# A 128-byte gap in SBUF between the weight ring and the activation pools of a transformer kernel

## The chip, the cores and the metric

The kernel runs on one core of one Trainium2 chip. The metric is device time in microseconds (us), lower is better: the median of three runs of the kernel before is 1367.99 us (1367.96 to 1368.49).

## What is computed

The input is one sequence of 256 tokens with 1024 features, all in fp32. It passes through a first block (a gated feed-forward network of width 2816; a mixer that joins a gated linear recurrence and windowed attention; a second feed-forward network) and then twice through a second kind of layer, with a convolution branch, a latent attention branch, a dilated attention branch and an output projection:

```python
def swiglu(x, w_gu, w_down):
    g, u = jnp.split(x @ w_gu, 2, axis=-1)
    return (jax.nn.silu(g) * u) @ w_down
...
        f = swiglu(rms_norm(h, ffn1_pre_g[l]), ffn1_w_gu[l], ffn1_w_down[l])
        h = h + MACARON_SCALE * rms_norm(f, ffn1_post_g[l])
        m = hybrid_mixer(rms_norm(h, mix_pre_g[l]), cos, sin, w_in[l], ...)
        h = h + rms_norm(m, mix_post_g[l])
...
    merged = g_a * (y_a @ w_out_a) + g_b * (y_b @ w_out_b) + g_c * (y_c @ w_out_c)
    return x + merged @ w_o
```

Nearly all of the arithmetic is in the products of the 256-token activations with weight matrices, 227 MB of weights in all, each used once.

## The kernel before, in words

**Matmuls.** Each fp32 product is done as three fp32r matmuls (`mm3`, L221 to L225): an operand x is split into a rounded high part and a remainder, and the kernel adds high*high (L223), high*low (L224) and low*high (L225) in PSUM. Every matmul loads its stationary operand afresh, so a stream of products is weight load, matmul, weight load, matmul, and so on, and the load for the next matmul runs beside the current one.

```python
m(out, lhsT=ah, rhs=bh, start=first, stop=False)
m(out, lhsT=ah, rhs=bl, start=False, stop=False)
self.last = m(out, lhsT=al, rhs=bh, start=False, stop=last).ins
```

`lhsT` is the stationary operand (128 columns, 512 bytes of each partition), `rhs` the moving one (256, 384, 416 or 512 columns of 4 bytes). There are two kinds of product:

- **Activation moves, weight stands** (`pairB`, L471): the moving operand is a row block of an activation tile (`xh`/`xl`, `ya`, `yb`, `yc`, `yl`), 256 columns wide, and the stationary one a 128-column slice of a weight unit. Products gu, gp, g, xg, bz, cx, zb and po.
- **Weight moves, activation stands** (`stepA` L429, `down` in `ffn` L529, `out_proj` L680): the moving operand is a weight unit, 384, 416 or 512 columns wide, and the stationary one a 128-token slice of an activation. Products dqk, uq (384), c (416), dn, o, ga, ua, q, kv, ukv (512).

**Weights.** A unit of weights comes by DMA from the SP queue into a ring of 4 raw buffers (`raw`), ScalarE writes its rounded high part (L206) and VectorE the remainder (L207) into one of 8 buffers of the weight ring (`w`, 8192 bytes each, high half first). At the end of a feed-forward network six units go into the pool `w2` in place of the ring, and in the output projections three units of eight go into buffers of the activation pools (`wb4`, `ws`). The trace drops trailing digits of names, so `w2` appears as `w` and `wb4` as `wb`.

**Order of the work.** A hand-kept clock (`tick`, `spawn`, `finish`) places the attention and recurrence work between the products; L_ORDER, M_ORDER and the costs W_* set the order. The order of instructions on every engine comes from this program and does not depend on addresses.

**Layout.** Pools are laid out in SBUF in the order in which `Kern.__init__` opens them: constants, `raw`, `w`, `sm` (small statistics), `b4` (4096 bytes each), `n`, `t`, `xT`, and then, phase by phase, the pools of that phase (`w2`, `l2`, `dil`, `s`, `pt`, `gth`, `c1`). All are whole multiples of 256 bytes per partition except the constants and `sm`: six tags of six buffers, padded to 32 or 64 bytes, 1344 bytes = 5 * 256 + 64. The byte addresses in each partition, in the layout of the compiled kernel before:

| what | address | address mod 256 |
|---|---|---|
| identity (for transposes, in the constants) | 9344 | 128 |
| weight ring `w`, first buffer | 32000 | 0 |
| `sm` | 97536 | 0 |
| `b4`, first buffer | 98880 | 64 |
| `xh`, `xl` | 156224, 164416 | 64 |
| pools of the phase (`w2`, `l2`, `dil`), first buffer | 172608 | 64 |

Steps inside a tile are multiples of 512 bytes for every matmul operand, with one exception: a weight row of the 416-wide chunk c is 1664 bytes = 6 * 256 + 128, so that its second row block (k = 1) starts at 128 mod 256, and its first (k = 0) at 0, in the high half and in the low half.

Of the kernel before, what the change touches and what calls it, by code (L numbers as in the profile page):

```python
# [10 lines left out]
F32 = mybir.dt.float32  # L11
# [5 lines left out]
P = 128  # L17
# [72 lines left out]
class Job:  # L90
# [3 lines left out]
    def __init__(self, gen, ready):  # L94
        self.gen, self.ready, self.done = gen, ready, False


class Kern:
    def __init__(self, tc, a, ex):
        self.tc, self.nc, self.a = tc, tc.nc, a  # L100
        pool = lambda name, bufs, **kw: ex.enter_context(tc.tile_pool(name=name, bufs=bufs, **kw))
        self.const = pool("const", 1)
        self.rawp = pool("raw", NRAW)
        self.wp = pool("w", NW)
        self.sm = pool("sm", 6)
        self.pools = {n: pool(n, k) for n, k in (("b4", NB4), ("n", NN), ("t", NT))}
        self.xp = pool("xT", 1)
        self.psum = pool("ps", 1, space=PSUM)
        self.now, self.live, self.last = 0.0, 0, None
        self.taken = deque([-W_X] * NX)  # L110
        self.lanes = {n: deque() for n in ("tp", "T", "S")}
# [1214 lines left out]
```

## Time and profile before

| what | value |
|---|---|
| median of three runs | 1367.99 us |
| the profiled execution's own time | 1368.98 us |
| its span, first to last instruction | 1367.2 us |
| PE busy with matmuls | 1339.2 us (98%) |
| PE weight loads (PEld) | 1236.1 us (90%) |
| VectorE, ScalarE busy | 950.1 us (69%), 780.5 us (57%) |
| DMA, mean | 168 GB/s |

Matmul records overlap one another (each lasts longer than the distance to the next), so their busy time says little; the distance from one matmul's start to the next one's is what a matmul costs in a stream. The timeline gives starts to 0.01 us, so a distance is read over a run of equal matmuls: last start less first start, divided by the number of steps.

### The profile page before, as it was taken

The numbers are of one execution on the slowest core, as the hardware profiler recorded it, in microseconds if no ns is written. First come the engines' busy times: TensorE is split into PE (matmuls) and PEld (weight loads), VectorE is DVE, ScalarE is ACT, GpSimd is POOL, SyncE is SP. The second block draws the span as 40 slices with busy tenths as digits, with TensorE's granted clock in tenths as the row PEclk, the third lists the DMA queues.
The fourth block names the chain that finished last, engine by engine and source line by source line (L and its number), as shares of the span: only waits on it lengthen the run. The fifth ranks groups of instructions, "written<-read, shape, count | busy, mean of one in ns | idle before, by whom it ended". The sixth has DMA issues, their size and how long they took to land.

```text
span 1367.2 us, 24721 instructions
## 1 busy us (share of the span) xinstructions
PE 1339.2 (98%) x9434; PEld 1236.1 (90%) x9434; DVE 950.1 (69%) x2178; ACT 780.5 (57%) x1464; POOL 3.0 (0%) x10
## 2 busy tenths in 40 slices
PE   7999999999999999999999999999999999999998
PEld 5999987888998899998998989999889989899997
DVE  6546667887878655558888676665788886766663
ACT  6444544787754544444667776454546667755451
POOL 0000000000000000000000000000000000000000
PEclk9999999999999999999999999999999999999999
DMA  7657764436565565673754454656556553556661
GB/s 257 220 165 226 227 210 150 122 115 156 166 207 183 176 192 186 201 229 86 218 139 123 129 170 124 184 172 187 174 160 176 150 133 96 174 157 178 186 183 49
DMA packets 234807, 230.30 MB, mean 168 GB/s; under 512 B 12336, under 2 KB 213184, under 8 KB 234688
## 3 DMA queue, kind: packets, MB, share of 16 engines
q1 hardware_dynamic: 232432, 227.05, 55.7%
q10 hardware_dynamic: 2256, 1.67, 0.5%
q8 instruction: 74, 1.21, 0.4%
q14 instruction: 45, 0.37, 0.1%
HBM read 227.64 MB, written 1.05 MB: 167 GB/s over the span
## 4 chain that ended last, share of the span: by engine, by line
PE 83%; DVE 8%; ACT 4%; DMA 3%; issue 2%; SPq 0%; ACTq 0%; DVEq 0%
PE gu L225 5%; PE gu L223 5%; PE gu L224 5%; PE dqk L223 4%; PE dqk L225 4%; PE dqk L224 4%; PE gp L223 3%; PE gp L225 3%; PE gp L224 3%; PE dn L223 3%; PE dn L225 3%; PE dn L224 3%; PE po L223 2%; PE po L225 2%; PE po L224 2%; PE sc L791 2%
## 5 line engine op out<-in xcount | busy, mean ns | idle before, releaser
L207 DVE TENSOR_TENSOR w<-raw,w 128x1024 fp32r<-128x1024 f32 (+1 forms) x437 | 502.4, 1157 | 234.1 <-ACT w L206 232.4
L206 ACT CAST w<-raw 128x1024 fp32r<-128x1024 f32 (+1 forms) x437 | 432.8, 999 | 348.6 <-PE gu L225 53.6
L223 PE MATMUL gu<-xh,w 128*128 128x256 f32 x576 | 161.4, 280 | 0.0
L225 PE MATMUL gu<-xh,w 128*128 128x256 f32 x576 | 161.1, 280 | 0.0
L224 PE MATMUL gu<-xl,w 128*128 128x256 f32 x576 | 160.7, 279 | 0.0
L223 PE MATMUL dqk<-w,xh 128*128 128x384 f32 x384 | 136.7, 356 | 3.0 <-ACT sq L1023 3.0
L224 PE MATMUL dqk<-w,xh 128*128 128x384 f32 x384 | 129.7, 338 | 0.0
L225 PE MATMUL dqk<-w,xl 128*128 128x384 f32 x384 | 129.3, 337 | 0.0
L223 PE MATMUL gp<-xh,w 128*128 128x256 f32 x384 | 109.2, 285 | 0.0
L224 PEld LDWEIGHTS gu<-xl,w 128*128 128x128 f32 x576 | 108.0, 188 | 0.7
L223 PEld LDWEIGHTS gu<-xh,w 128*128 128x128 f32 x576 | 107.9, 187 | 0.7
L225 PEld LDWEIGHTS gu<-xh,w 128*128 128x128 f32 x576 | 108.2, 188 | 0.0
L224 PE MATMUL gp<-xl,w 128*128 128x256 f32 x384 | 107.2, 279 | 0.0
L225 PE MATMUL gp<-xh,w 128*128 128x256 f32 x384 | 107.1, 280 | 0.0
L223 PEld LDWEIGHTS dqk<-w,xh 128*128 128x128 f32 x384 | 72.1, 188 | 9.9 <-issue 6.0
L223 PEld LDWEIGHTS gp<-xh,w 128*128 128x128 f32 x384 | 72.0, 187 | 3.1 <-issue 2.7
L224 PEld LDWEIGHTS dqk<-w,xh 128*128 128x128 f32 x384 | 72.3, 188 | 0.2
L224 PEld LDWEIGHTS gp<-xl,w 128*128 128x128 f32 x384 | 72.2, 188 | 0.0
L225 PEld LDWEIGHTS dqk<-w,xl 128*128 128x128 f32 x384 | 72.1, 188 | 0.0
L225 PEld LDWEIGHTS gp<-xh,w 128*128 128x128 f32 x384 | 71.9, 188 | 0.0
L223 PE MATMUL dn<-w,aT 128*128 128x512 f32 x176 | 69.2, 393 | 0.0
L224 PE MATMUL dn<-w,aT 128*128 128x512 f32 x176 | 69.2, 393 | 0.0
(377 smaller groups left out, 3245.8 us busy)
## 6 DMA issues: line engine op xcount, KB each, us to landing
raw<-in_w_in_dram SPq DMA_DIRECT2D x140, 512.0 KB
raw<-in_ffn_w_gu_dram SPq DMA_DIRECT2D x88, 512.0 KB
raw<-in_w_in_dram SPq DMA_DIRECT2D x192, 192.0 KB
raw<-in_ffn_w_down_dram SPq DMA_DIRECT2D x44, 512.0 KB
raw<-in_w_o_dram SPq DMA_DIRECT2D x16, 512.0 KB
raw<-in_w_proj_attn_dram SPq DMA_DIRECT2D x16, 256.0 KB
raw<-in_w_proj_lru_dram SPq DMA_DIRECT2D x8, 512.0 KB
raw<-in_w_out_dram SPq DMA_DIRECT2D x8, 512.0 KB
```

What stands on the lines that cost most here:

```text
L206: nc.scalar.copy(hi, raw)
L207: nc.vector.tensor_tensor(lo, raw, hi, op=ALU.subtract)
L223: m(out, lhsT=ah, rhs=bh, start=first, stop=False)
L224: m(out, lhsT=ah, rhs=bl, start=False, stop=False)
L225: self.last = m(out, lhsT=al, rhs=bh, start=False, stop=last).ins
L791: self.nc.tensor.matmul(p[:, c], lhsT=q[:, cq], rhs=k[:, ck], start=True, stop=True)
```

## The change

A pool of one buffer of 32 fp32 values (128 bytes in each partition) is opened after the weight ring. Its tile is never written or read, so no instruction is added, and the instructions and their order stay. Every pool opened after it (`sm`, `b4`, `n`, `t`, `xT` and the pools of all phases) starts 128 bytes higher; constants, `raw` and `w` stay.

```diff
@@ -102,6 +102,8 @@
         self.const = pool("const", 1)
         self.rawp = pool("raw", NRAW)
         self.wp = pool("w", NW)
+
+        pool("gap", 1).tile([P, 32], F32, name="gap")
         self.sm = pool("sm", 6)
         self.pools = {n: pool(n, k) for n, k in (("b4", NB4), ("n", NN), ("t", NT))}
         self.xp = pool("xT", 1)
```

## Rows read from the trace of the kernel before

**Rows 1.** The page: span, PE's busy time, and TensorE's granted clock in 40 slices

```profile
span 1367.2 us, 24721 instructions
PE 1339.2 (98%) x9434; PEld 1236.1 (90%) x9434; DVE 950.1 (69%) x2178; ACT 780.5 (57%) x1464; POOL 3.0 (0%) x10
PEclk9999999999999999999999999999999999999999
```

**Rows 2.** The page: the chain that ended last, shares by engine

```profile
PE 83%; DVE 8%; ACT 4%; DMA 3%; issue 2%; SPq 0%; ACTq 0%; DVEq 0%
```

**Rows 3.** Windows: stretch, length, busy of PE, PEld, DVE, ACT, POOL, clock, DMA

```profile
906.20:972.20 66.00, 66.00 (x562) 66.00 (x562) 40.61 (x43) 33.87 (x46) 0.00 (x0) 1.00 0.63 191
```

**Rows 4.** Timeline of PE, that stretch's first and last matmul: start, duration, instruction

```profile
906.20 0.28 PE L224 MATMUL gp<-xl,w 128*128 128x256 f32 x1
...
972.27 0.28 PE L225 MATMUL po<-ych,w 128*128 128x256 f32 x1
```

**Rows 5.** Timeline of PE, feed-forward tail: units of the ring, then of `w2`

```profile
182.66 0.39 PE L223 MATMUL dn<-w,aT 128*128 128x512 f32 x1
...
183.36 0.39 PE L223 MATMUL dn<-w,aT 128*128 128x512 f32 x1
...
185.42 0.39 PE L223 MATMUL dn<-w,aT 128*128 128x512 f32 x1
...
186.10 0.39 PE L223 MATMUL dn<-w,aT 128*128 128x512 f32 x1
```

**Rows 6.** Timeline of PE, the 416-wide chunk: starts of its triples, k = 1 first

```profile
998.00 0.35 PE L223 MATMUL c<-w,xh 128*128 128x416 f32 x1
...
998.57 0.35 PE L223 MATMUL c<-w,xh 128*128 128x416 f32 x1
...
999.13 0.35 PE L223 MATMUL c<-w,xh 128*128 128x416 f32 x1
...
999.70 0.35 PE L223 MATMUL c<-w,xh 128*128 128x416 f32 x1
...
1000.26 0.35 PE L223 MATMUL c<-w,xh 128*128 128x416 f32 x1
...
1000.83 0.35 PE L223 MATMUL c<-w,xh 128*128 128x416 f32 x1
...
1001.39 0.35 PE L223 MATMUL c<-w,xh 128*128 128x416 f32 x1
```

**Rows 7.** One line's instructions, L223: count, duration min/median/max, first and last start

```profile
L223 PE MATMUL gu<-xh,w x576: 278/279/392, 38.0 to 602.7; 128*128 128x256 f32 x192
L223 PE MATMUL dqk<-w,xh x384: 332/336/531, 626.9 to 1174.7; 128*128 128x384 f32 x192
L223 PE MATMUL gp<-xh,w x384: 276/279/392, 806.4 to 1335.2; 128*128 128x256 f32 x192
L223 PE MATMUL dn<-w,aT x176: 388/394/398, 50.4 to 624.3; 128*128 128x512 f32 x176
L223 PE MATMUL xg<-xh,w x128: 276/280/388, 240.3 to 352.4; 128*128 128x256 f32 x128
...
L223 PE MATMUL po<-ybh,w x64: 279/279/387, 823.6 to 1221.4; 128*128 128x256 f32 x64
...
L223 PE MATMUL o<-w,mT x60: 393/394/501, 413.2 to 1358.6; 128*128 128x512 f32 x60
L223 PE MATMUL ga<-w,xh x32: 388/396/796, 11.4 to 455.8; 128*128 128x512 f32 x32
...
L223 PE MATMUL c<-w,xh x32: 346/352/460, 626.5 to 1011.9; 128*128 128x416 f32 x32
```

**Rows 8.** Timeline of PE, a short stretch of xg after a break

```profile
282.32 0.28 PE L223 MATMUL xg<-xh,w 128*128 128x256 f32 x1
...
283.79 0.28 PE L224 MATMUL xg<-xl,w 128*128 128x256 f32 x1
```

**Rows 9.** One line's instructions, L773: transposes with the identity as moving operand

```profile
L773 PE MATMUL pT<-ident,s x240: 270/272/328, 259.6 to 1252.4; 128*128 128x128 f32 x120
```

## The prediction

> **What bounds the kernel now.** I read the page first: PE is at 98% of the span and its granted clock is full, the 2.4 GHz level, in every slice [rows 1]. A full PE row alone does not prove that PE is the bound, because matmul records overlap, so the chain comes second: 83% of the time of the chain that ended last lies on PE, 8% on VectorE, 4% on ScalarE, 3% on DMA [rows 2]. Third come windows: in 66.00 us of gp and po products PE and the weight loads are both busy without a gap, while VectorE works 40.6 us, ScalarE 33.9 us and the DMA engines 63% [rows 3]. There nothing but the pace of the matmuls sets the time. That pace is the number to look at: 561 steps from 906.20 to 972.27 us, 117.8 ns each [rows 4]. The parts below count 8,232 matmuls of the split products, so one nanosecond on each is 8 us.
>
> **What of the pace depends on addresses.** The change adds no instruction, no wait and no DMA. It can act only through where tiles lie. The trace has two places where the same instruction runs at two paces and only the address of an operand differs.
>
> The first is the tail of a feed-forward network. Three steps of dn with weights of the ring take 183.36 - 182.66 = 0.70 us, or 233 ns each; a few matmuls later, same shape, same line, same activations as stationary operand, three steps with weights of `w2` take 186.10 - 185.42 = 0.68 us, or 227 ns [rows 5]. The ring lies at 0 mod 256 and `w2`, like the activations, at 64.
>
> The second is the 416-wide chunk, whose weight rows lie alternately at 128 (k = 1) and 0 (k = 0) mod 256 while the activations stay at 64. The triples take 0.57, 0.56, 0.57, 0.56, 0.57, 0.56 us [rows 6]: the three of k = 1 together 1.71 us, those of k = 0 together 1.68 us, so 190.0 against 186.7 ns, 3.3 ns per matmul.
>
> So I take the pace to depend on the **offset**: where the moving operand starts, less where the weight load beside it (the next matmul's stationary operand) starts, mod 256 bytes. In these terms the rows say: offset 0 (`w2`) is cheapest, offset 192 (0 - 64: ring weights moving, k = 0) costs more, offset 64 (128 - 64: k = 1) costs 3.3 ns more than 192. That it is 256 and not a larger period I take from the chunk itself, where high and low half of a row lie 256 apart mod 512 and stand in the same short triple.
>
> **The change by parts.** Only operands that move against each other count. The activation pools go from 64 to 192, the ring stays at 0.
>
> A. *Activation moves, ring weight stands.* Offset 64 - 0 = 64 before, 192 after. Counts of line 223 [rows 7]: gu 576, gp 384, five groups of 128 like xg, five of 64 like po, together 1,920; three lines, 5,760 matmuls. No row shows 256-wide matmuls at offset 192. The bounds: the best pace that they show anywhere is 13 steps in 283.79 - 282.32 = 1.47 us, 113.1 ns, in short stretches of the same products at the same offset [rows 8]; so a gain of at most 4.7 ns. From the other side, a loss as large as the offset has been seen to make, 3.3 ns. I take a gain of 3.3 ns, because the chunk is the nearest row: the only one that shows offsets 64 and 192 side by side. 5,760 * 3.3 = 19.0 us less. PE stands on the path in these products [rows 3], so it is worth nearly its full size there.
>
> B. *Ring weight moves, activation stands.* Offset 192 before, 64 after. Of 384 columns dqk 384 and uq 16 on each line, 1,200 in all; of 512 columns dn 176 less the 48 that read `w2`, o 60, three groups of 32 like ga, kv 16 and ukv 8, that is 308 on each line and 924 in all [rows 7]. The price is the chunk's with the sign turned, +3.3 ns; bounds 0 (a wider matmul could absorb it) and 6.7 ns (the whole difference that an offset makes in [rows 5], once more). 2,124 * 3.3 = 7.0 us more.
>
> C. *The 416-wide chunk.* 96 matmuls; k = 0 and k = 1 change places [rows 6, 7]: zero.
>
> D. *Both operands in activation pools* (dn from `w2`, o from `wb4` and `ws`: 84 on each line, 252; also the scores and the products with probabilities). Both move alike: zero.
>
> E. *Transposes.* The identity stays at 128, its partner goes from 64 to 192: offset 64 becomes 192. There are 528, of which 240 on line 773 [rows 9]. By the chunk's price at most 1.7 us either way; I take zero, since they lie in gaps with other waits.
>
> F. *ScalarE, VectorE, DMA.* The splits read `raw` and write the ring, which stay. The rest of their work moves by 128 bytes; no row shows a duration that would depend on that, and the slack of [rows 3] covers it. If a ScalarE or VectorE step did get slower, the 12% of the chain that is theirs is where it would show.
>
> Sum: -19.0 + 7.0 = -12.0 us of matmul pace. Not all of it reaches the end: some stretches wait for a load or for an evacuation, and a faster stream reaches those waits sooner. The share of the chain that is PE's, 83% [rows 2], turns 12.0 into 10.0. Against the profiled execution's own 1368.98 us that is 1359.0; the median of the runs is 1.0 lower, so the forecast is **1358.0 us**, 0.7% faster. What is late next is the weight feed: DMA at 63% in the stretch of [rows 3] leaves room for a stream that is 3% faster.
>
> One rule of the Trainium skill speaks against any effect. TensorE: Matmul & The Clock Gate, "Part 2: What happens when you issue a matmul", has it that PE reads its moving operand and its weight loads through two independent ports and that "Loading the next tile's weights doesn't steal SBUF read bandwidth from the running matmul." By it the time would stay at 1368; [rows 5] do not agree as far as they go, 233 against 227 ns for one instruction. That result is the third rival.
>
> **The rivals.**
>
> *1. The wide ones lose and the narrow ones don't gain: slower.* In 256-wide products the weight load fills the whole step: PEld is busy 66.00 of 66.00 us [rows 3]. If the load and not the moving read sets those 117.8 ns, the offset could leave them alone, while part B, where the moving read is longer than the load, pays its 7.0 us. That gives 1368.0 + 7.0 = 1375.0 us. It decides when the narrow matmuls gain less than 7.0 us / 5,760 = 1.2 ns. For it: B's price is measured on moving weights, A's is borrowed. Against it: the same products run at 113.1 ns in places [rows 8], so the load alone does not need 117.8.
>
> *2. The other sign.* What counts might be the moving operand's own address, or the order in which the two reads meet, and 256 columns could answer to 192 as 416 do to 64: a loss on PE passes in full, a gain by its 83%, so 1368.0 + 19.0 - 5.8 = 1381 us. For it: the price in [rows 6] was never seen on a moving activation. Against it: offset 0 is cheapest and both rows can be put in one order, 0, 192, 64, without any other variable.
>
> *3. Nothing.* The activations stand 64 bytes off a 128-byte grid before and after; if that grid is what matters, or if each stream settles into the same pace whatever the offset, the time stays at 1368.0. For it: the pace in [rows 4] is the same over 561 steps and several tiles. Against it: k = 0 and k = 1 differ by exactly 128 bytes and do not run alike [rows 6].
>
> *4. The full gain.* A falls to the 113.1 ns of [rows 8] and B stays: 5,760 * 4.7 = 27 us of pace, 83% of it 22, so 1346 us.
>
> **How the numbers follow.** Forecast 0.46, rival 1 0.20, rival 2 0.08, rival 3 0.13, rival 4 0.13. About 0.2% (2.7 us) is what a measurement of this kernel can tell from no change. Faster: forecast and rival 4, less a little of the forecast that may shrink into the band, 0.58. Same: rival 3 and that little, 0.14. Slower: rivals 1 and 2, 0.28. The range must hold the forecast with its bounds and most of rivals 1, 3 and 4: 1346 to 1375. Left out are rival 2 and the far halves of 1 and 4, about 0.2. Cases of both signs have weight; the forecast's own range is 1351 to 1365, by A between half and all of its 4.7 ns and B between 0 and 7 us.
>
> **What would show it.** Right: the timeline's 256-wide step in gp falls from 117.8 to about 114.5 ns, the 512-wide ring step of dn rises from 233 to about 237, dn from `w2` stays at 227, and in the 416-wide chunk the triples change places. Rival 1: the first stays and the second rises. Rival 3: neither moves, and the chunk's triples do not change places. If the wide steps fall and the narrow ones rise, the offset is the wrong variable. If the steps move as forecast and the time does not, the gain has gone into waits for DMA, which the chain would then show above 3%.

## The result: 1.1% faster, and the profile after

The changed kernel takes 1353.45 us (median of six runs, 1347.91 to 1355.79) against 1368.13 us (six runs, 1367.96 to 1370.23): a ratio of 0.9886, with a 95% interval of 0.9868 to 0.9905. The forecast was 1358.0 us, range 1346 to 1375. The profiled execution took 1355.79 us.

The page after, with the lines that answer to [rows 1, 2]:

```profile
span 1354.0 us, 24721 instructions
PE 1325.1 (98%) x9434; PEld 1224.6 (90%) x9434; DVE 950.2 (70%) x2178; ACT 780.3 (58%) x1464; POOL 3.0 (0%) x10
PEclk9999999999999999999999999999999999999999
...
PE 80%; DVE 7%; ACT 6%; DMA 4%; issue 2%; SPq 0%; ACTq 0%; DVEq 0%
```

As many instructions as before, the same granted clock, VectorE and ScalarE as busy as before to 0.2 us. All of the difference is on PE, whose matmuls and weight loads are each some 12 to 14 us less busy. The two added lines of the diff move line numbers by two: `mm3` is L225 to L227 here.

The timeline of PE after, first and last start of three stretches of 256-wide products (start us, duration us, instruction); each last row is the first matmul behind its stretch:

```profile
147.07 0.28 PE L225 MATMUL gu<-xh,w 128*128 128x256 f32 x1
...
180.99 0.40 PE L225 MATMUL dn<-w,aT 128*128 128x512 f32 x1
...
564.13 0.28 PE L225 MATMUL gu<-xh,w 128*128 128x256 f32 x1
...
596.80 0.39 PE L225 MATMUL dn<-w,aT 128*128 128x512 f32 x1
...
896.55 0.28 PE L227 MATMUL gp<-xh,w 128*128 128x256 f32 x1
...
962.63 0.40 PE L225 MATMUL o<-w,mT 128*128 128x512 f32 x1
```

The first stretch has 288 steps in 33.92 us, 117.8 ns each, the pace of before [rows 4]. The second, the same 288 products in the second feed-forward network, takes 32.67 us: 113.4 ns each, the pace that before the change showed only in short pieces [rows 8]. The third, 561 steps of gp and po, is at 117.8 again. So one program, one offset, two paces.

The wide products, in the same view: dn from the ring, and the 416-wide chunk by its triples, k = 0 first:

```profile
127.50 0.39 PE L225 MATMUL dn<-w,aT 128*128 128x512 f32 x1
...
129.56 0.39 PE L225 MATMUL dn<-w,aT 128*128 128x512 f32 x1
...
999.07 0.35 PE L225 MATMUL c<-w,xh 128*128 128x416 f32 x1
...
999.64 0.35 PE L225 MATMUL c<-w,xh 128*128 128x416 f32 x1
...
1000.21 0.35 PE L225 MATMUL c<-w,xh 128*128 128x416 f32 x1
...
1000.78 0.35 PE L225 MATMUL c<-w,xh 128*128 128x416 f32 x1
...
1001.34 0.35 PE L225 MATMUL c<-w,xh 128*128 128x416 f32 x1
...
1001.91 0.35 PE L225 MATMUL c<-w,xh 128*128 128x416 f32 x1
```

dn makes nine steps in 2.06 us, 229 ns, where it made 233 [rows 5]: faster, not slower. In the chunk k = 0 and k = 1 have changed places, as their offsets have (k = 0 now at 0 - 192 = 64, k = 1 at 128 - 192 = 192): the three triples of k = 0 take 0.57 us each, 190 ns a step, the two of k = 1 between them 0.57 and 0.56 us, some 188 ns (all by starts rounded to 0.01 us); in [rows 6] k = 1 was the dearer one.

### The profile page after: what moved, and what is told of

It reads as the page before. It is cut to its first block, busy times and chain, and to the rows that moved or that the text cites. A ratio compares the mean times of both kernels' runs of the same rounds, so it can differ in the third digit from the quotient of the medians.

```text
span 1354.0 us, 24721 instructions
## 1 busy us (share of the span) xinstructions
PE 1325.1 (98%) x9434; PEld 1224.6 (90%) x9434; DVE 950.2 (70%) x2178; ACT 780.3 (58%) x1464; POOL 3.0 (0%) x10
## 4 chain that ended last, share of the span: by engine, by line
PE 80%; DVE 7%; ACT 6%; DMA 4%; issue 2%; SPq 0%; ACTq 0%; DVEq 0%
PE gu L225 5%; PE gu L226 5%; PE gu L227 5%; PE dqk L225 4%; PE dqk L227 4%; PE dqk L226 4%; PE gp L225 4%; PE gp L226 3%; PE gp L227 3%; PE dn L227 3%; PE dn L226 3%; PE dn L225 3%; PE sc L793 2%; PE po L225 2%; DMA raw<-in_w_in_dram 2%
## 5 line engine op out<-in xcount | busy, mean ns | idle before, releaser
L225 PE MATMUL gu<-xh,w 128*128 128x256 f32 x576 | 160.5, 279 | 0.0
L227 PE MATMUL gu<-xh,w 128*128 128x256 f32 x576 | 160.1, 278 | 0.0
L225 PE MATMUL dqk<-w,xh 128*128 128x384 f32 x384 | 136.7, 356 | 2.7 <-ACT sq L1025 2.7
L227 PE MATMUL dqk<-w,xl 128*128 128x384 f32 x384 | 129.0, 337 | 0.0
L225 PE MATMUL gp<-xh,w 128*128 128x256 f32 x384 | 109.9, 286 | 0.0
L227 PEld LDWEIGHTS gu<-xh,w 128*128 128x128 f32 x576 | 109.0, 189 | 0.0
L225 PEld LDWEIGHTS gu<-xh,w 128*128 128x128 f32 x576 | 108.1, 188 | 0.7
L227 PE MATMUL gp<-xh,w 128*128 128x256 f32 x384 | 107.2, 280 | 0.0
L225 PEld LDWEIGHTS dqk<-w,xh 128*128 128x128 f32 x384 | 72.2, 188 | 9.6 <-issue 6.0
L225 PEld LDWEIGHTS gp<-xh,w 128*128 128x128 f32 x384 | 73.1, 190 | 3.5 <-issue 2.7
L227 PEld LDWEIGHTS dqk<-w,xl 128*128 128x128 f32 x384 | 72.1, 188 | 0.0
L227 PEld LDWEIGHTS gp<-xh,w 128*128 128x128 f32 x384 | 72.1, 188 | 0.0
L227 PE MATMUL dn<-w,aT 128*128 128x512 f32 x176 | 69.0, 392 | 0.0
```

## The experiments

All are edits of the kernel before, so that its line numbers hold (`mm3` is L223 to L225). The theory was the prediction's: the pace of a matmul depends on the offset mod 256 between the moving operand and the weight load beside it. Below, "mean step" is the mean distance between the starts of successive matmuls of one class, over all steps that no break interrupts (those over 126, 186, 200 and 241 ns for 256, 384, 416 and 512 columns are left out): some 5,490, 1,010, 80 and 870 steps in each trace; those of 512 columns are the ring's alone, without `w2`, `wb4` and `ws`. Offsets are given as 256-wide (activation moving) / wide (ring weight moving).

### Relation or own address: the gap ahead of the ring

```diff
-        self.rawp = pool("raw", NRAW)
+        self.rawp = pool("raw", NRAW); pool("gap", 1).tile([P, 32], F32, name="gap")
```

> The gap is put ahead of the weight ring instead of behind it, so the ring and the activations both lie 128 bytes higher and their offset is that of the kernel before (64 with an activation moving, 192 with a ring weight moving). Theory, offset between the two reads: nothing changes, 1368 us within 3 us, 256-wide products at 117.8 ns, 512-wide ones from the ring at 233.3. Rival, the activations' own address: it is the same here as in the changed kernel (192 mod 256), so 1353 us, with stretches of 256-wide products at 113.5 ns.

Measured: ratio 0.9995 (0.9985 to 1.0005). The gp stretch in the timeline of this run:

```profile
906.51 0.28 PE L225 MATMUL gp<-xh,w 128*128 128x256 f32 x1
...
972.59 0.40 PE L223 MATMUL o<-w,mT 128*128 128x512 f32 x1
```

561 steps, 117.8 ns; ring products 512 wide at 233.3. The activations lie where they lie in the changed kernel, and nothing is gained. The activations' own address is out as the cause; their distance from the ring is in. (One long stretch of po in this trace ran at 113.3 ns; the others kept 117.8.)

### The period: a gap of 256 bytes

```diff
+        pool("gap", 1).tile([P, 64], F32, name="gap")
```

> A gap of 256 bytes behind the ring in place of 128. Theory, offset mod 256: the kernel before again, 1368 us within 3 us, 117.8 ns and 233.3 ns. Rival, a longer period (512 or more): another time than 1368, and other paces. Rival, any move of the activations frees something (banks, DMA, the other engines): near 1353.

Measured: ratio 1.0005 (0.9996 to 1.0015); mean steps 117.7, 174.6 and 233.3 ns, those of the kernel before (117.7, 174.7, 233.3). So a period of 256 bytes fits, and none of its smaller divisors does, since the change itself is a move by 128. That everything moves is not what helps.

### Offset 0: a gap of 192 bytes

```diff
+        pool("gap", 1).tile([P, 48], F32, name="gap")
```

> A gap of 192 bytes: activations and ring both lie at 0 mod 256, offset 0 for every product. Theory, offset: 512-wide products from the ring fall from 233.3 to the 227 ns that the w2 units show (some 900 of them, 6 us), 384-wide ones to 172 ns (2 to 3 us), 256-wide ones to between 113.5 and 115.5 ns (13 to 24 us): 1336 to 1348 us. Rival, the activations' own address: the 512-wide ones from the ring stay at 233 or 229 and the time lies between 1353 and 1368.

Measured: ratio 1.0037 (1.0025 to 1.0049), 1375.5 us: slower, where 1336 to 1348 was expected. The timeline shows which part of the expectation held: six steps of dn with ring weights, nine with `w2`, and the gp stretch.

```profile
182.73 0.39 PE L223 MATMUL dn<-w,aT 128*128 128x512 f32 x1
...
184.09 0.39 PE L223 MATMUL dn<-w,aT 128*128 128x512 f32 x1
...
186.13 0.39 PE L223 MATMUL dn<-w,aT 128*128 128x512 f32 x1
...
909.99 0.29 PE L225 MATMUL gp<-xh,w 128*128 128x256 f32 x1
...
977.30 0.40 PE L223 MATMUL o<-w,mT 128*128 128x512 f32 x1
```

Ring: 1.36 us / 6 = 227 ns; `w2`: 2.04 us / 9 = 227 ns. The difference of [rows 5] is gone once the ring has the offset of `w2`, in the same instructions, on the same engine, in the same stage. But the 256-wide steps are at 67.31 us / 561 = 120.0 ns, dearer than at 64, and the 384-wide ones, expected at 172, have a mean step of 174.4, next to 174.7 before. The offset that is best for 512 columns is bad for 256, and there are six times as many of those.

### Offset 128: a gap of 64 bytes

```diff
+        pool("gap", 1).tile([P, 16], F32, name="gap")
```

> A gap of 64 bytes: activations at 128 mod 256, offset 128 in both kinds of product. Theory, offset: an offset not seen so far; the pace of every class moves away from the kernel before, 256-wide between 113.5 and 122 ns, 512-wide between 227 and 240; if half a period is the worst place, 1380, if it lies between its neighbours 64 and 192, 1360. Rival, nothing but the 128-byte shift matters: 1368.

Measured: ratio 1.0046 (1.0030 to 1.0063), 1377.3 us. This is near the 1380 that was set for half a period as the worst place. Mean steps 118.9, 176.1 and 232.5 ns; the long 256-wide stretches sit at 118.7 or at 120.0 ns, again two paces. "Only the 128-byte shift matters" falls.

### The changed kernel once more

> The changed kernel once more, for a second trace of the same program. Theory, at offset 192 a stretch of 256-wide products takes one of two paces (113.5 or 117.8 ns) when it starts and keeps it: the time is 1348 to 1356 us, every long stretch shows one of the two paces and nothing between, and some stretches show the other one than in the first trace. Rival, the pace is fixed by the place in the program: the same stretches show the same pace as before (113.6 in gu from 45 to 90 us, 117.8 from 100 to 181, 117.8 in both gp stretches).

Measured: ratio 0.9885 (0.9858 to 0.9912); 1350.95 to 1358.86 us, one run of four above the 1356 that was expected at most. The gp stretch of this trace, and both gp stretches of the last run of the study (below), which has the same offsets:

```profile
895.77 0.28 PE L225 MATMUL gp<-xh,w 128*128 128x256 f32 x1
...
959.37 0.39 PE L223 MATMUL o<-w,mT 128*128 128x512 f32 x1
```

```profile
899.49 0.28 PE L225 MATMUL gp<-xh,w 128*128 128x256 f32 x1
...
965.57 0.40 PE L223 MATMUL o<-w,mT 128*128 128x512 f32 x1
...
1265.58 0.28 PE L225 MATMUL gp<-xh,w 128*128 128x256 f32 x1
...
1329.17 0.39 PE L223 MATMUL o<-w,mT 128*128 128x512 f32 x1
```

Here gp takes 63.60 us, 113.4 ns a step, where the first trace of the same offsets had 66.08 us and 117.8. The gu stretches between 100 and 176 us are at 113.4 to 113.6 here and at 117.8 there, and xg at 337 us the other way round. In the last run one gp stretch is slow (66.08 us) and its twin in the next layer fast (63.59 us). So the program alone does not fix the pace: a long stretch has one of the two from its start and keeps it until the stream is broken, and six of the 17 stretches of 90 steps or more differ between these two traces.

Nor is every stretch open. Four traces have these offsets: the first, this one, the last run and the padded kernel with the 128-byte gap below. In all four, 11 of the 17 stretches show the same pace: ten are always fast, among them all long gu stretches of the second feed-forward network, and the po stretch near 385 us is always slow. Of the other six, the three gu stretches between 100 and 181 us changed together in these traces; the rest are xg and the two gp stretches. The traces come from more than one chip, so execution and chip are not told apart, and what decides at the start is not shown.

### Between the multiples of 64: gaps of 96 and 160 bytes

```diff
+        pool("gap", 1).tile([P, 24], F32, name="gap")
```

In the second kernel the tile is [P, 40].

> Gap of 96 bytes: offset 160 with an activation moving, 96 with a ring weight moving. Theory, the pace changes with the offset in steps of 64 or less: 256-wide between the neighbours' 119 (offset 128) and 115.5 (192), 512-wide between 229.7 (64) and 231.7 (128): 1353 to 1376 us. Rival, only the 64-byte part counts (160 behaves as 128): 1377 us. Rival, 160 has the fast pace alone: 113.5 ns and about 1340 us.

> Gap of 160 bytes: offset 224 with an activation moving, 32 with a ring weight moving. Theory, between the neighbours: 256-wide between 115.5 (192) and 119.9 (0), 512-wide between 227.5 (0) and 229.7 (64): 1350 to 1374 us. Rival, 224 has the fast pace alone: 113.5 ns and about 1338 us.

Measured: ratios 1.0022 (1.0010 to 1.0034) and 1.0045 (1.0028 to 1.0062). At 160 the 256-wide stretches sit at 117.3 or 118.7 ns, at 224 all of them at 118.3 to 118.4. The wide ones rise to 233.5 (offset 96) and 233.3 (offset 32), outside the neighbours that were expected to enclose them (by the ring alone the neighbours are 229.7 and 232.5 for the first, 227.7 and 229.7 for the second). The 160-byte gap, at 1375.2 us, is 1.2 us above the top of its range, as much as the kernel before was slower beside it than in the first comparison (1369.3 against 1368.1 us). So the pace at one offset cannot be read off its neighbours 32 bytes away.

### Steps of 16 bytes

Pools start at multiples of 32 bytes in the compiled layout, so `xh` and `xl` were put in one tile and read from its fifth element on; that moves 4,800 of the 5,760 256-wide products. It moves more: the wide products in which `xh` or `xl` stands, and, as the tile is 32 bytes longer, the pools of the phases by 32 bytes. So the paces can be compared, while the times mix several offsets. Gap 128 bytes in the first kernel, 96 in the second.

```diff
+        x = self.xp.tile([P, 16 * S + 8], F32R, tag="xh", name="xh")[:, 4:4 + 16 * S]
+        x = x.rearrange("p (j k s) -> p j k s", j=2, k=8)
+        return x[:, 0], x[:, 1]
```

> Gap of 128 bytes, and xh/xl (in one tile) start 16 bytes further on: offset 208 for 4,800 of the 5,760 256-wide products. Theory, the pace moves in steps of 16 bytes (one more or less conflict between the two reads): a pace for gu, gp, xg, bz that is neither 113.4 nor 117.8, or one of them alone in every stretch. If the fast pace is alone: 1346 us. Rival, only 32 bytes and more count: the two paces of offset 192 again, 1348 to 1358 us.

> The same from the other side: gap of 96 bytes and xh/xl 16 bytes further on, offset 176 (products po at 160 as with the 96-byte gap, 117.4 ns). Theory, steps of 16 bytes: a pace of its own, between 113.4 and 118.7 ns; fast alone would give 1352 us, as the po and the 512-wide products are dearer here than at 128. Rival, only 32 bytes and more count: as with the 96-byte gap, 117.3 or 118.7 ns, 1372 us.

Measured in one run each: 1369.3 and 1375.2 us, beside 1372.1 for the kernel before. The gu stretch at offset 208:

```profile
567.77 0.28 PE L223 MATMUL gu<-xh,w 128*128 128x256 f32 x1
...
602.09 0.39 PE L223 MATMUL dn<-w,aT 128*128 128x512 f32 x1
```

288 steps in 34.32 us, 119.2 ns, in every gu stretch; at 176 it is 119.2 to 119.3. In gu, sixteen bytes to either side of 192 cost all of the gain in pace, so "only 32 bytes and more count" falls. The Trainium skill, SBUF — State Buffer, "Door 1: The DMA port swizzle", says that SBUF has lines of 16 bytes and that an access that crosses to a new line pays. A shift by 16 bytes leaves an operand's place within its line as it was, so that rule alone does not give the difference, and no run here shows whether lines are the cause.

The first of the two runs holds one more test of the offset. Its aT lies at 192 mod 256 and its `w2`, 32 bytes further, at 224: dn from the ring (offset 64) has a mean step of 228.7 ns, and dn from `w2` (offset 32 in place of 0) 233.1 ns; with the 128-byte gap alone they have 229.2 and 227.6. The dearer one changes places with the offset.

### Why the chunk misled: rows of whole 256 bytes

```diff
-            w = p.tile([P, 2, kt, cols], F32R, tag=pool, name=pool)
+            w = p.tile([P, 2, kt, 448 if cols == 416 else cols], F32R, tag=pool, name=pool)[:, :, :, 0:cols]
```

Without a gap (all 96 matmuls at offset 192), and with the 128-byte gap (all at 64):

> No gap; the rows of the 416-wide chunk in the ring are padded to 448 columns (1792 bytes, a whole number of 256), so that all its 96 matmuls have offset 192 instead of 192 and 64 in turn. Theory, the difference of 3.3 ns within the chunk belongs to the offset: all at 186.7 to 187.6 ns. Rival, it belongs to the turn from one offset to the other: a single pace for all, but another one. The time stays at 1368 us either way (96 matmuls of 3 ns are 0.3 us).

> The changed kernel with the chunk's rows padded to 448 columns, so that its 96 matmuls all have offset 64 (the counterpart, all at 192, ran at 186.7 ns). Theory, turning from one offset to the other makes the chunk's difference: a steady offset of 64 costs no more than 192 here too, 187 ns or less, as in the 384- and 512-wide products (173.2 against 174.7, 229.7 against 233.3). Rival, the width 416 itself: 190 ns, as in the mixed chunk. Time 1350 to 1356 us either way.

The chunk in both traces, 18 steps from one triple's start to another's:

```profile
1007.50 0.35 PE L223 MATMUL c<-w,xh 128*128 128x416 f32 x1
...
1010.86 0.35 PE L223 MATMUL c<-w,xh 128*128 128x416 f32 x1
```

```profile
997.75 0.35 PE L223 MATMUL c<-w,xh 128*128 128x416 f32 x1
...
1001.14 0.35 PE L223 MATMUL c<-w,xh 128*128 128x416 f32 x1
```

3.36 us / 18 = 186.7 ns at 192 and 3.39 us / 18 = 188.3 ns at 64 (times 1368.8 and 1356.2 us in one run each). The first expectation held; in the second neither did. A steady offset of 64 is cheaper than the 190 ns of the mixed chunk, so by these two traces about half of the 3.3 ns belonged to the turns from one offset to the other; the other half, 1.6 ns, is there without any turn and has the opposite sign from what 384 and 512 columns show.

### The best version, timed

> The best version of the study (gap of 128 bytes, chunk rows padded to 448 columns) timed in five rounds. Theory, two paces at offset 192 chosen anew in every execution: ratio 0.985 to 0.991 to the kernel before, and single times that spread over more than 5 us, with those of the kernel before on the same chip within about half of that; the trace again shows a mixture of 113.5 and 117.8 ns of its own. Rival, the mixture is the program's: the same stretches as in the first trace of this kernel (gu fast throughout, both gp stretches slow) and a spread no wider than that of the kernel before.

Measured: ratio 0.9891 (0.9870 to 0.9912), 1350.0 to 1356.8 us. Its trace has the two paces in another mixture than the first trace of the same kernel (the padded one above): four of the 17 long stretches differ, the three gu between 100 and 181 us and the second gp. So the rival falls there. The spread, 6.7 us, was not wider than that of the kernel before on that chip (1362.9 to 1371.1), so on that point the expectation failed. It does not beat the changed kernel; no version tried does.

### All offsets in one table

| kernel | offsets | 256 wide, mean step ns | long 256-wide stretches, ns | 384 | 512 (ring) | ratio |
|---|---|---|---|---|---|---|
| before | 64 / 192 | 117.7 | 117.8 | 174.7 | 233.3 | 1 |
| gap ahead of ring | 64 / 192 | 117.5 | 117.8, one at 113.3 | 175.0 | 233.3 | 0.9995 |
| gap 64 | 128 / 128 | 118.9 | 118.7 or 120.0 | 176.1 | 232.5 | 1.0046 |
| gap 96 | 160 / 96 | 117.8 | 117.3 or 118.7 | 176.6 | 233.5 | 1.0022 |
| **gap 128, changed** | 192 / 64 | 115.5 | 113.4 to 113.6, or 117.8 | 173.2 | 229.7 | 0.9886 |
| gap 128, again | 192 / 64 | 114.3 | 113.4 to 113.6, or 117.8 | 173.2 | 229.3 | 0.9885 |
| gap 160 | 224 / 32 | 118.3 | 118.3 | 174.4 | 233.3 | 1.0045 |
| gap 192 | 0 / 0 | 119.8 | 119.9 to 120.0 | 174.4 | 227.7 | 1.0037 |

## Why the prediction was right, and where it was not

**The bound and the variable: right.** The time follows the pace of the matmuls, and the pace follows the offset between ring and activations: shown by the gap ahead of the ring (same activations' address, no gain), by 256 bytes (no gain) and by offset 0 (ring and `w2` alike at 227 ns). What in the chip makes the offset matter stays open. The rule cited from the Trainium skill (TensorE: Matmul & The Clock Gate, "Part 2: What happens when you issue a matmul"), two ports that do not disturb each other, would have given no change; these fp32r streams do not agree with it, as one instruction takes 227, 229 or 233 ns by the offset alone. Whether the operand that matters is the load for the next matmul or the matmul's own weights was not separated, since the ring's buffers agree mod 256.

**Part A: right in sign, mis-sized.** Taken: 3.3 ns on each of 5,760. Measured in the profiled execution: 117.7 to 115.5, 2.2 ns over 5,495 undisturbed steps, 12.0 us of pace. What the step missed is that offset 192 has no single price. It allows the 113.4 ns of [rows 8] to hold for a whole stretch, or 117.8 as before; 2.2 is the mixture in that execution, 3.4 in the second trace. What was named as showing it right, gp at about 114.5 ns, did not come in the profiled execution: both its long gp stretches stayed at 117.8, and the gain lies in other stretches. The prediction read the stretch of [rows 8] as a bound; it was the second pace, which at offset 64 too turns up now and then, and at 192 in 11 to 15 of the 17 long stretches of a trace. That the sign came out right is in part luck: it was borrowed from the same chunk that misled part B.

**Part B: wrong in sign.** The step that failed is "The price is the chunk's with the sign turned, +3.3 ns". The 384-wide products fell from 174.7 to 173.2 and the 512-wide from 233.3 to 229.7 ns: 1,014 * 1.5 + 866 * 3.7 = 4.7 us less, where 7.0 more were forecast; dn from the ring, named to rise to about 237 ns, fell to 229. The padded rows show why the chunk was a bad witness: about half of its difference came from alternating, and the rest has the other sign from that of 384 and 512 columns. With it falls the order 0, 192, 64 that the prediction set up across widths, and the 192-byte gap showed what trusting such an order costs: +0.4%.

**Parts C, D, F: right.** The triples changed places; dn from `w2` has a mean step of 227.2 ns before and 227.6 after; VectorE's and ScalarE's busy times stayed. E, the transposes, was not told apart.

**The sum.** Pace: 12.0 + 4.7 = 16.7 us. Between the profiled executions 1368.98 - 1355.79 = 13.2 us arrived, 79%; 83% was taken. The forecast of 10.0 us was thus near by luck: A's gain was sized too high by 7 us and B was off by 12 us to the other side. Where the remaining 21% went is not shown in full: the distances between matmul starts that are not undisturbed steps of the split products (breaks, changes of shape, the small matmuls) add up to 254 us before and 259 after, but which waits grew was not followed. DMA's share of the chain is 4% after 3%, though runs that gained nothing show 4% or 5% too, so that share alone proves little. The 83% is no firm figure either: the kernel with the 256-byte gap, with the paces of the kernel before, shows 80%.

**The range.** The forecast's own range, 1351 to 1365, does not come out of the bounds named for it: A between 13.5 and 27 us less and B between 0 and 7 us more, at 83%, give 1346 to 1363. The measured 1353.45 us lies in both.

**The rivals.** Rival 1 (narrow ones unmoved, wide ones dearer) and 2 fell with B's sign and A's. Rival 3 fell by the ratio. Rival 4's pace is nearly that of the fast stretches (113.4 to 113.6 ns); no trace had it in all.

## What to carry to other kernels

When a stream of fp32r matmuls with a fresh weight load each is the bound, the byte distance between the two SBUF operands, mod 256, is worth a scan, in steps of 32 bytes or less: in this kernel it moves the time from -1.1% to +0.5% without touching an instruction. Take each width's price from that width in an undisturbed stream; a price from another width, or from a place where offsets alternate, can have the wrong sign. And read the distance between starts over long stretches, not busy time or a mean: with two paces in one stage, single executions can differ.

## What the runs showed that was not expected

- Two paces at one offset: 113.4 and 117.8 ns for 256 columns at offset 192 (118.7 and 120.0 at 128, 117.3 and 118.7 at 160), there from the start of a stretch, kept over up to 561 steps, and in six of 17 long stretches not the same in every trace.
- Sixteen bytes of displacement between the two operands raise the step of gu from 113.4 or 117.8 to 119.2 ns, on either side of 192.
- The best offset depends on the width: 192 for 256 columns, 64 for 384, 0 for 512 of those tried.
